# The second projection of a hybrid decoder layer, w_out: half of its inner dimension by Strassen's seven products

## The chip, the core and the metric

The kernel is one program on one core of a Trainium2 chip. Work is done by TensorE (matmuls, PE in the profile, with PEld for the loads of the stationary operand), VectorE (DVE), ScalarE (ACT) and GpSimd (POOL); SyncE (SP) issues most of the transfers from the chip's memory. Each engine works through its own queue of instructions in the order of the built program, and waits at an instruction until what it needs is there. The metric is the device time of one execution in microseconds (us).

## The reference

One decoder layer on 256 tokens of width 1024, all in float32. The part that matters here is the end of the middle sub-layer and the beginning of the last one:

```python
gates = jax.nn.sigmoid(gate_logits + gate_b[l]).reshape(b, L, N_BRANCH, D_MODEL)
merged = gates[:, :, 0] * y_ssd + gates[:, :, 1] * y_att
h = h + rmsnorm(merged @ w_out[l], mix_post_g[l])
h = h + 0.5 * rmsnorm(swiglu(rmsnorm(h, ffn2_pre_g[l]), ffn2_w_gate[l], ffn2_w_up[l], ffn2_w_down[l]),
                      ffn2_post_g[l])
```

`merged` is 256 x 1024 and `w_out` is 1024 x 1024. `y_att` is itself a product with `da_w_branch`.

## The kernel before

**Numbers in two parts.** Every product is made of three: an operand x is split into a rounded part hi (a copy to the type fp32r) and the rest lo = x - hi, and hi*hi, lo*hi and hi*lo are added up in PSUM. For a weight chunk, 1 MB in a raw buffer (`raw`, three of them, filled by SP), ScalarE makes the hi part (`whi`, line 259) and VectorE the lo part (`wlo`, line 260), each in two pieces of 128 x 1024. A raw buffer is free when the second lo piece is made; then SP issues the load of the chunk three further on. `take()` gives the next chunk's two parts and sees that the chunks up to AHEAD = 3 further on are split.

**The stage.** Tokens lie in two blocks b of 128, channels of the output in two halves q of 512. After the attention, `natural("pwd0")` and `natural("pwd1")` multiply with `da_w_branch` (tiles `pwd`, line 382); `merge` (lines 1612, 1613) gates the result and adds the other branch into `gt`; `turn_merged` transposes a block of `merged` on TensorE (tiles `pmg`, line 1596) and splits it into `mh` and `ml` (lines 320, 321). Then `mm_n` multiplies with the four chunks of `w_out` (tiles `acc_mx`, line 676): the first chunk for both blocks and both halves, the other three (held back, TAIL = 3) block by block, half by half, so that a half of a block is done early. Per chunk, block and half there are six matmuls of 512 columns, 96 in all. As each half is done, `norm_half` takes its sum of squares on ScalarE (`jp_mxp`, line 506) and multiplies it by the gain on VectorE (`og_mxp`, line 605); `norm_end` gets the root on GpSimd (`rp_mxp`, lines 511 and 512) and adds to the residual `h` on VectorE (line 645).

**What follows.** For the next sub-layer block 0 of `h` is transposed as it is (`pu_f`, line 520, between matmuls of block 1), split into `u_f` (lines 526, 528) and multiplied with the first four chunks of that sub-layer's weights (tiles `pn_f`, line 382), with its norm applied later. Block 1 of `h` is squared on ScalarE (`sq_f`, line 506), its root is taken on GpSimd (`r_f`, lines 511, 512), VectorE scales it (`un_f`, line 565), and TensorE transposes it (`pu_f` again) after three quarters of block 0's product, that is 36 matmuls of `pn_f`.

**What sets the order.** In this stretch the order of TensorE's queue is the one in which the code is written. ACT's and DVE's queues are ordered by the scheduler of the framework at build time, under a few added constraints: `normed["lo"]` names an instruction behind which the later `wlo` pieces have to stand.

The sub-layers with SwiGLU already use Strassen's scheme for parts of their last product: class `Quad` holds two chunks as four quarters, makes weight sums (`SUMS`), and `mm_quads` runs seven products instead of eight blocks, followed by sums of the results (lines 784 and 787 to 792). `sums_of` makes the sums of the activations.

## Time and profile before

| | us |
|---|---|
| median of 3 runs | 731.69 (731.35 to 731.74) |
| the profiled execution | 731.22 |
| its span, first to last instruction | 729.3 |
| PE busy | 721.3 |
| DVE busy | 608.5 |
| ACT busy | 472.8 |
| the product with `w_out`, first matmul to the first of `pn_f` | 519.71 to 543.36 |

The span lies 1.9 us under the time of the same execution. A row of the timeline has the start and the length in us, the engine, the line, the operation, what it writes and reads, its shape, how many were merged into the row, and in brackets how long the engine was idle before it and what it waited for. The second start in a row of n equal instructions is not shown; the interval between them is the row's length less that of one, divided by n - 1. In the chain of work that ended last, a row is start, length, engine, tile, line and count.

### The profile page before, as it was taken

The page shows a single profiled execution, that of the slowest core. Times are in us where ns is not written, and L with a number is a line of the kernel's source. Part 1 is how long each engine was busy: PE and PEld are TensorE (multiplying, and loading weights), DVE is VectorE, ACT ScalarE, POOL GpSimd, SP SyncE. Part 2 cuts the span into 40 slices and gives each one's busy share as a digit, 9 for nine tenths or more (in the row PEclk, how much of TensorE's full clock was granted, in tenths as well). Part 3 has the DMA queues.
Part 4 walks back from the last instruction along what each step waited for, and adds up shares of the span by engine and source line. Part 5 has one row for each costly group of instructions (what it writes and reads, how often), then busy time and mean ns, then how long its engine had stood idle before and what let it go on. Part 6 is the DMA issues. An engine that isn't in the chain of part 4 may idle for free.

```text
span 729.3 us, 10568 instructions
## 1 busy us (share of the span) xinstructions
PE 721.3 (99%) x4025; PEld 620.5 (85%) x4025; DVE 608.5 (83%) x933; ACT 472.8 (65%) x804; POOL 31.5 (4%) x63
## 2 busy tenths in 40 slices
PE   9999999999999999999999999999999999999996
PEld 8888888888778889999888788888888888888885
DVE  6978788999979989777996998785784878789996
ACT  6657666666867676869965577782563756566562
POOL 4300000000200000000000000000010000000000
PEclk9999999999999999999999999999999999999998
DMA  8884654467674557665564664465461655654551
GB/s 303 229 275 153 208 173 176 170 231 260 185 227 119 172 173 238 208 213 180 155 224 147 205 224 137 152 235 199 120 234 51 230 182 166 231 194 156 174 197 58
DMA packets 94450, 137.92 MB, mean 189 GB/s; under 512 B 2668, under 2 KB 68800, under 8 KB 94400
## 3 DMA queue, kind: packets, MB, share of 16 engines
q1 hardware_dynamic: 91728, 129.51, 53.7%
q0 software_dynamic: 2368, 7.22, 3.3%
q8 instruction: 31, 0.51, 0.3%
q10 hardware_dynamic: 304, 0.53, 0.2%
q14 instruction: 19, 0.16, 0.1%
HBM read 136.17 MB, written 1.08 MB: 188 GB/s over the span
## 4 chain that ended last, share of the span: by engine, by line
PE 95%; DVE 2%; DMA 1%; issue 1%; ACT 0%; DVEq 0%; ACTq 0%
PE pup_f L341 14%; PE pg_f L341 14%; PE pxs L341 6%; PE pws L382 6%; PE pgt L382 6%; PE acc_f2p L755 5%; PE acc_f1p L755 3%; PE pbc L341 3%; PE pk L341 3%; PE pq L341 3%; PE pn_f L398 3%; PE acc_mx L676 3%; PE pn_mx L382 3%; PE pn_f L382 3%; PE pwd L382 3%; PE pz L333 2%
## 5 line engine op out<-in xcount | busy, mean ns | idle before, releaser
L260 DVE TENSOR_TENSOR wlo<-raw,whi 128x1024 fp32r<-128x1024 f32 x216 | 257.0, 1219 | 20.2 <-ACT whi L259 19.0
L259 ACT CAST whi<-raw 128x1024 fp32r<-128x1024 f32 x216 | 218.4, 1049 | 16.1 <-DMA raw<-in_w_in_dram 5.7
L341 PE MATMUL pg_f<-u_f,whi 128*128 128x512 f32 x288 | 69.0, 390 | 0.0
L341 PE MATMUL pup_f<-u_f,whi 128*128 128x512 f32 x288 | 68.7, 391 | 0.0
L341 PEld LDWEIGHTS pg_f<-u_f,whi 128*128 128x128 f32 x288 | 53.9, 188 | 11.1
L341 PEld LDWEIGHTS pup_f<-u_f,whi 128*128 128x128 f32 x288 | 52.9, 188 | 10.2
L130 ACT CAST wqh<-wt 128x1024 fp32r<-128x1024 f32 x24 | 25.2, 1055 | 23.5 <-DVE wt L122 23.4
L341 PEld LDWEIGHTS pg_f<-u_f,wlo 128*128 128x128 f32 x288 | 36.9, 191 | 1.4
L341 PE MATMUL pup_f<-u_f,wlo 128*128 128x256 f32 x288 | 37.5, 283 | 0.0
L341 PE MATMUL pg_f<-u_f,wlo 128*128 128x256 f32 x288 | 37.4, 283 | 0.0
L347 ACT COPY su_f<-pup_f 128x256 f32<-128x256 f32 x36 | 13.2, 372 | 36.1 <-PE pup_f L341 36.1
L341 PEld LDWEIGHTS pup_f<-u_f,wlo 128*128 128x128 f32 x288 | 35.9, 192 | 0.0
L348 DVE TENSOR_TENSOR su_f<-pup_f,su_f 128x256 f32<-128x256 f32 x36 | 15.2, 421 | 24.2 <-ACT su_f L347 24.1
L382 PE MATMUL pgt<-whi,u_mx 128*128 128x512 f32 x128 | 33.1, 393 | 0.0
L341 PE MATMUL pxs<-u_mx,whi 128*128 128x512 f32 x128 | 31.8, 394 | 0.0
L330 PE MATMUL pz<-u_mx,whi 128*128 128x256 f32 x128 | 31.6, 284 | 0.0
L331 PE MATMUL pz<-u_mx,whi 128*128 128x256 f32 x128 | 31.5, 283 | 0.0
L136 DVE TENSOR_TENSOR wql<-wt,wqh 128x1024 fp32r<-128x1024 f32 x24 | 29.1, 1217 | 0.2
L382 PEld LDWEIGHTS pgt<-whi,u_mx 128*128 128x128 f32 x128 | 23.6, 188 | 5.3 <-issue 0.7
L341 PEld LDWEIGHTS pxs<-u_mx,whi 128*128 128x128 f32 x128 | 23.2, 189 | 4.3
L320 ACT CAST gh_f<-sg_f 128x512 fp32r<-128x512 f32 x18 | 11.2, 620 | 23.2 <-DVE sg_f L911 23.2
L136 DVE TENSOR_TENSOR wql<-raw,wqh 128x1024 fp32r<-128x1024 f32 x18 | 21.8, 1219 | 3.5 <-ACT wqh L130 3.5
(415 smaller groups left out, 1585.1 us busy)
## 6 DMA issues: line engine op xcount, KB each, us to landing
raw<-in_w_in_dram SPq DMA_DIRECT2D x40, 1024.0 KB, 5.1
raw<-in_ffn_w_down_dram SPq DMA_DIRECT2D x22, 1024.0 KB, 4.9
raw<-in_ffn_w_gate_dram SPq DMA_DIRECT2D x20, 1024.0 KB, 5.4
raw<-in_ffn_w_up_dram SPq DMA_DIRECT2D x20, 1024.0 KB, 5.2
raw<-in_ssd_w_branch_dram SPq DMA_DIRECT2D x8, 1024.0 KB, 5.0
acb<-acd POOLq DMA_DIRECT2D x8, 512.0 KB, 4.1
raw<-in_da_w_branch_dram SPq DMA_DIRECT2D x4, 1024.0 KB, 5.1
raw<-in_w_out_dram SPq DMA_DIRECT2D x4, 1024.0 KB, 5.1
```

Source lines behind the costliest of these rows:

```text
L130: nc.scalar.copy(hi, src)
L136: nc.vector.tensor_sub(lo, src, hi.bitcast(F32))
L259: last_cast[0] = behind(nc.scalar.copy(hi, r[:, js, :]), "cast").ins
L260: m = nc.vector.tensor_sub(lo, r[:, js, :], hi.bitcast(F32))
L330: nc.tensor.matmul(acc[m], wh(j)[:, cs], ah(k0 + j), start=first and j == ks[0], stop=False)
L331: nc.tensor.matmul(acc[m], wh(j)[:, cs], al(k0 + j), start=False, stop=False)
L341: nc.tensor.matmul(to, w_(j)[:, m * P:(m + 1) * P], x_(j), start=first and j == 0, stop=not first and j == KD - 1, skip_group_check=True)
L348: nc.vector.tensor_tensor(dst, acc[:, :T], dst, ALU.add)
L382: nc.tensor.matmul(acc, a(k0 + j), b(j), start=first and i == 0, stop=last and i == 11)
L398: nc.tensor.matmul(accs[b], x_(k0 + j), w_(j), start=first and j == 0 and w_ is wh and x_ is acts[b][0], stop=last and j == 3 and w_ is wl)
L676: nc.tensor.matmul(acc[b][q][:, cs] if to is None else to, x_[:, ts], w_(kt)[:, halves[q]][:, cs], start=to is not None and kt == 0 and x_ ...
L755: nc.tensor.matmul(bank[p], x_, w_, start=p not in begun, stop=last and p in (1, 5, 6, 7))
```

## The change

The first 512 of the 1024 inner channels of the product with `w_out` are computed by seven products of quarter size (each 128 tokens x 256 channels x 512 outputs, six matmuls) instead of eight. The other two chunks ("plain" chunks) stay as they were. In detail:

- The two chunks 85 and 86 become a `Quad` with the order of products 1, 2, 6, 5, 3, 7, 4. Of the seven weight operands three are quarters of the chunks themselves and four are sums, made on VectorE into one tile `wt_mx` with room for two at a time (it has the tag `u8`, that of the activation buffers that stand idle here); each of the seven is then split (`wqh` on ScalarE, `wql` on VectorE).
- Six of the seven are made ahead, during the products with `da_w_branch`; the sixth in order, product 7, among them, and the seventh, 4, in the middle of the product with `w_out`.
- The merged activations' first half is turned block by block inside `natural("pwd1")`, copied once more in plain form (`mt`) and summed by `sums_of` (`sv`, `sh`, `sl`, `s4`).
- The seven results lie in eight banks of PSUM with the plain chunks' parts and are merged by adds: `p1` copied by ScalarE, `u2`, `u4`, `u3`, `c4` on VectorE, and one more add per half (`half_mixed`) before that half's norm, which then reads its input from SBUF.
- The `wlo` pieces of the next sub-layer's chunks stand behind the second half's add of block 0 (`normed["lo"]`), and those of chunks 91 and 92 are asked for after the halves of block 1.

```diff
@@ -48,6 +48,7 @@
+MIXED = (1, 2, 6, 5, 3, 7, 4)
...
@@ -97,8 +98,8 @@
-        def __init__(self, i, products):
-            self.i, self.sums, self.products = i, {}, products
+        def __init__(self, i, products, homes=None):
+            self.i, self.sums, self.products, self.homes = i, {}, products, homes

...
@@ -118,7 +119,7 @@
             if p not in self.sums:
                 n, m = self.SUMS[p]
                 m = self.sum_of(m) if p in (6, 4) else self.quarter(m, p)
-                t = k4([P, 2, 512], f"wt{self.i}{p}")
+                t = self.homes(p) if self.homes else k4([P, 2, 512], f"wt{self.i}{p}")
                 nc.vector.tensor_sub(t, self.quarter(n, p), m)
                 self.sums[p] = t
             return self.sums[p]
...
@@ -213,8 +214,19 @@
     for c in range(2):
         for k0 in (0, 512):
             s_chunk(da_w_branch[0], k0, c * 512)
-    for c in range(4):
+    sums_home = []
+
+    def mixed_home(p):
+
+        if not sums_home:
+            sums_home.append(sb.tile([P, 4, 2, T], F32, tag="u8", name="wt_mx", bufs=2))
+        return sums_home[0].rearrange("p (a b) c t -> p a b (c t)", a=2)[:, {5: 0, 6: 1, 7: 0, 4: 1}[p]]
+
+    quad(w_out[0], 0, MIXED, mixed_home)
+    last_unit_mx = units.pop()
+    for c in range(2, 4):
         n_chunk(w_out[0], c * 2 * P)
+    units.append(last_unit_mx)
     ffn_chunks("f2", ffn2_w_gate, ffn2_w_up, ffn2_w_down)
 
     raws, splits = [], []
...
@@ -742,6 +754,78 @@
         split(more[:, 0], more[:, 1], v[:, 3])
         return ([hi[:, i] for i in range(3)] + [more[:, 0]], [lo[:, i] for i in range(3)] + [more[:, 1]])
 
+    def of_piece(p, kt, acts, sh, sl):
+
+        if p in (1, 2, 4):
+            k, b = {1: (0, 0), 2: (2, 0), 4: (2, 1)}[p]
+            return [x_[:, b * P:(b + 1) * P] for x_ in acts[k + kt]]
+        return [x_[{5: 0, 6: 1, 7: 2, 3: 3}[p]][:, kt, :] for x_ in (sh, sl)]
+
+    def mm_mixed(acts, sums, turn_next, half, done, turned):
+
+
+        bank, begun = {}, set()
+        sh, sl = sums
+        rest = {n: k2([P, 512], f"{n}_mx") for n in ("p1", "u2", "u4", "u3", "c4")}
+        add = lambda o, p, u: nc.vector.tensor_tensor(rest[o], bank[p], rest[u], ALU.add)
+
+        def mm(p, x_, w_, stop):
+            nc.tensor.matmul(bank[p], x_, w_, start=p not in begun, stop=stop)
+            begun.add(p)
+
+        def piece(p, w):
+            if p not in bank:
+                bank[p] = pj(f"acc_mxp{p}") if p in (1, 6, 7, 4) else bg([P, 512], f"acc_mxp{p}")
+            wh, wl = w
+            for kt in range(2):
+                ah, al = of_piece(p, kt, acts[:4], sh, sl)
+                for x_, w_ in ((ah, wh), (al, wh), (ah, wl)):
+                    mm(p, x_, w_(kt), kt == 1 and w_ is wl and p in (1, 5, 6, 7))
+
+        def plain(b, q, p, i, w, at):
+            wh, wl = w
+            for kt in range(2):
+                if (i, kt) == at:
+                    turned()
+                ah, al = (x_[:, b * P:(b + 1) * P] for x_ in acts[4 + 2 * i + kt])
+                for x_, w_ in ((ah, wh), (al, wh), (ah, wl)):
+                    mm(p, x_, w_(kt)[:, halves[q]], i == 1 and kt == 1 and w_ is wl)
+
+        def part(b, q, p, ws, o, at=None):
+            for i, w in enumerate(ws):
+                plain(b, q, p, i, w, at)
+            return half(b, q, bank[p], rest[o])
+
+        split_to(taken[0] + 7)
+        piece(1, take(0))
+        nc.scalar.copy(rest["p1"], bank[1])
+        piece(2, take(0))
+        piece(6, take(0))
+        turn_next()
+        add("u2", 6, "p1")
+        piece(5, take(0))
+        turn_next()
+        add("u4", 5, "u2")
+        piece(3, take(0))
+        w7 = take(0)
+        ws = [take(1) for _ in range(2)]
+        split_to(taken[0] + 1)
+        w4 = take(0)
+        part(0, 0, 2, ws, "p1")
+        normed["lo"] = part(0, 1, 3, ws, "u4")
+        done(0)
+        split_to(ahead_of(taken[0], AHEAD - 2))
+        split_to(ahead_of(taken[0], AHEAD - 1))
+        piece(7, w7)
+        add("u3", 7, "u2")
+        add("c4", 5, "u3")
+        piece(4, w4)
+        bank[8] = pj("acc_mxp8")
+        part(1, 0, 4, ws, "u3", at=(1, 1))
+        part(1, 1, 8, ws, "c4")
+        split_to(ahead_of(taken[0], AHEAD))
+        done(1)
+
     def mm_quads(acts, sums, tag):
 
 
...
@@ -1541,18 +1621,20 @@
 
     own_order(PE)
 
-    def natural(name, n, hi, lo, evict, us, then=lambda: None):
+    def natural(name, n, hi, lo, evict, us, then=lambda: None, ahead={}, behind_block=lambda i: None):
 
 
         accs = [pj(f"{name}{b}") for b in range(2)]
         for i in range(n):
-            w = take()
+            w = take(2 if i in ahead else AHEAD)
+            split_to(taken[0] + ahead.get(i, 0))
             for b in range(2):
                 bs = slice(b * P, (b + 1) * P)
                 mm_nat(accs[b], w, (lambda k: hi(k)[:, bs], lambda k: lo(k)[:, bs]), i * 4, i == 0, i == n - 1, "u")
                 if i == n - 1:
                     evict(b, accs[b])
                 back.run(us)
+                behind_block(i)
             if i == 0:
                 then()
 
...
@@ -1586,49 +1668,64 @@
     yh = yl = None
     while turned_pairs[0] < 2:
         back.run(0.1)
-    mg, merges = [], []
+    mg, merges, turned_halves, plain_mg, sums_mg = [], [], [], [], []
 
     def turn_merged(n):
 
-        for q, b, t, mh, ml in merges[:n]:
+        for q, b, t in merges[:n]:
+            if len(turned_halves) == q:
+                turned_halves.append([k4([P, 4, T], f"m{x_}{q}", F32R) for x_ in "hl"])
+                mg.extend((turned_halves[q][0][:, m, :], turned_halves[q][1][:, m, :]) for m in range(4))
+            mh, ml = turned_halves[q]
             pt = bg([P, 4, P], f"pmg{q}{b}")
             for m in range(4):
                 nc.tensor.transpose(pt[:, m, :], t[:, m * P:(m + 1) * P], ident)
             bs = slice(b * P, (b + 1) * P)
             split(mh[:, :, bs], ml[:, :, bs], pt)
+            if q == 0:
+                nc.scalar.copy(plain_mg[0][:, :, bs], pt)
         del merges[:n]
 
     def attended():
         back.drain()
         act_table(SILU)
 
+    def turn_block(i):
+        if i == 0:
+            turn_merged(1)
+            if not merges:
+                sums_mg.append(sums_of(0, plain_mg[0][:, 0:2, :], plain_mg[0][:, 2:4, :]))
+
     for q in range(2):
-        mh = k4([P, 4, T], f"mh{q}", F32R)
-        ml = k4([P, 4, T], f"ml{q}", F32R)
-        mg += [(mh[:, m, :], ml[:, m, :]) for m in range(4)]
-
         def merge(b, acc):
             t0, t1 = gt[0][b][:, halves[q]], gt[1][b][:, halves[q]]
             nc.vector.tensor_tensor(t1, acc, t1, ALU.mult)
-            nc.vector.tensor_tensor(t1, t1, t0, ALU.add)
-            merges.append((q, b, t1, mh, ml))
-
+            m = nc.vector.tensor_tensor(t1, t1, t0, ALU.add)
+            if (q, b) == (1, 0):
+                normed["lo"] = m.ins
+            merges.append((q, b, t1))
+
+        if q == 1:
+            plain_mg.append(k4([P, 4, T], "mt"))
         natural(f"pwd{q}", 2, lambda j: oh[j // 4][:, j % 4, :], lambda j: ol[j // 4][:, j % 4, :], merge,
-                SSD_US if q == 0 else 0.0, (attended, lambda: turn_merged(2))[q])
+                SSD_US if q == 0 else 0.0, (attended, lambda: None)[q], ({}, {0: 7, 1: 6})[q],
+                (lambda i: None, turn_block)[q])
 
     pg = load_gain(mix_post_g, "pg_mx")
-    acc = [[bg([P, 512], f"acc_mx{b}{q}") for q in range(2)] for b in range(2)]
 
     made, ready, turned = next_norm("f2", "f2")
+    norms_mx = [{}, {}]
+
+    def half_mixed(b, q, acc, rest):
+        m = nc.vector.tensor_tensor(rest, acc, rest, ALU.add)
+        norm_half(norms_mx[b], b, q, rest, pg, 1.0, "mxp")
+        return m.ins
 
     def mixed(b):
-        n = {}
-        for q in range(2):
-            norm_half(n, b, q, acc[b][q], pg, 1.0, "mxp")
-        norm_end(n, b, 1.0, "mxp")
+        norm_end(norms_mx[b], b, 1.0, "mxp")
         ready(b)
 
-    mm_n(acc, mg, mixed, turned, lambda: turn_merged(1))
+    mm_mixed(mg, sums_mg[0], lambda: turn_merged(1), half_mixed, mixed, turned)
 
 
     norm = made[0]
```

What it does to the queues, at three places. The names are those of the two builds; chunk 90 is `raw90`, its pieces `wlo900` and `wlo901`.

DVE, from the first half of block 1's norm (`og_mxp10`) to the scaled block 1 (`un_f211`), before:

```order
L605 TENSOR_TENSOR og_mxp10_5457<-acc_mx10_5242,pg_mx_5238 128x512
L528 SCALAR_TENSOR_TENSOR u0_f2_5352<-pu_f200_5392,cols_a_112,u0_f2_5352 128x128 x4
L528 SCALAR_TENSOR_TENSOR u1_f2_5353<-pu_f201_5405,cols_a_112,u1_f2_5353 128x128 x4
L260 TENSOR_TENSOR wlo920_5483<-raw92_5362,whi920_5482 128x1024
L260 TENSOR_TENSOR wlo921_5487<-raw92_5362,whi921_5486 128x1024
L605 TENSOR_TENSOR og_mxp11_5461<-acc_mx11_5243,pg_mx_5238 128x512
L645 SCALAR_TENSOR_TENSOR h_72<-og_mxp10_5457,rp_mxp1_5463,h_72 128x512
L645 SCALAR_TENSOR_TENSOR h_72<-og_mxp11_5461,rp_mxp1_5463,h_72 128x512
L565 TENSOR_SCALAR un_f210_5476<-h_72,r_f21_5473 128x512
L565 TENSOR_SCALAR un_f211_5478<-h_72,r_f21_5473 128x512
```

And in the changed kernel, from the same instruction on:

```order
L617 TENSOR_TENSOR og_mxp10_5478<-u3_mx_5269,pg_mx_5264 128x512
L617 TENSOR_TENSOR og_mxp11_5495<-c4_mx_5270,pg_mx_5264 128x512
L272 TENSOR_TENSOR wlo910_5498<-raw91_5343,whi910_5497 128x1024
L272 TENSOR_TENSOR wlo911_5502<-raw91_5343,whi911_5501 128x1024
L657 SCALAR_TENSOR_TENSOR h_72<-og_mxp10_5478,rp_mxp1_5507,h_72 128x512
L657 SCALAR_TENSOR_TENSOR h_72<-og_mxp11_5495,rp_mxp1_5507,h_72 128x512
L272 TENSOR_TENSOR wlo920_5527<-raw92_5399,whi920_5526 128x1024
L272 TENSOR_TENSOR wlo921_5531<-raw92_5399,whi921_5530 128x1024
L577 TENSOR_SCALAR un_f210_5520<-h_72,r_f21_5517 128x512
L577 TENSOR_SCALAR un_f211_5522<-h_72,r_f21_5517 128x512
```

Between the gain of the last half and the update of `h` now stand `wlo910` and `wlo911`, and `wlo920` and `wlo921` between `h` and `un_f`.

Ahead of that, DVE in the changed kernel from the second half of block 0 on (`u4`, which is line 1720; the results of products 7, 5, 4 and 8 are `acc_mxp7` and so on):

```order
L1720 TENSOR_TENSOR u4_mx_5268<-acc_mxp3_5328,u4_mx_5268 128x512
L272 TENSOR_TENSOR wlo890_5392<-raw89_5176,whi890_5391 128x1024
L617 TENSOR_TENSOR og_mxp01_5382<-u4_mx_5268,pg_mx_5264 128x512
L272 TENSOR_TENSOR wlo891_5396<-raw89_5176,whi891_5395 128x1024
L657 SCALAR_TENSOR_TENSOR h_72<-og_mxp00_5365,rp_mxp0_5384,h_72 128x512
L657 SCALAR_TENSOR_TENSOR h_72<-og_mxp01_5382,rp_mxp0_5384,h_72 128x512
L272 TENSOR_TENSOR wlo900_5402<-raw90_5279,whi900_5401 128x1024
L272 TENSOR_TENSOR wlo901_5406<-raw90_5279,whi901_5405 128x1024
L770 TENSOR_TENSOR u3_mx_5269<-acc_mxp7_5411,u2_mx_5267 128x512
L540 SCALAR_TENSOR_TENSOR u0_f2_5389<-pu_f200_5437,cols_a_112,u0_f2_5389 128x128
L770 TENSOR_TENSOR c4_mx_5270<-acc_mxp5_5313,u3_mx_5269 128x512
L540 SCALAR_TENSOR_TENSOR u0_f2_5389<-pu_f200_5437,cols_a_112,u0_f2_5389 128x128 x3
```

From here to `og_mxp10` above stand four more of `u1_f2` and two adds of line 1720 (`u3_mx` with `acc_mxp4`, `c4_mx` with `acc_mxp8`). Before, `og_mxp00`, two `wlo`, `og_mxp01` and two `h` stood in this place, followed by `og_mxp10`.

ACT, the last halves' sums of squares and the squares of `h`, before:

```order
L506 ACTIVATE jp_mxp10_5455,sp_mxp1_5454<-acc_mx10_5242 128x512
L526 ACTIVATE u0_f2_5352<-pu_f200_5392,cols_a_112 128x128 x4
L526 ACTIVATE u1_f2_5353<-pu_f201_5405,cols_a_112 128x128 x4
L259 CAST whi920_5482<-raw92_5362 128x1024
L259 CAST whi921_5486<-raw92_5362 128x1024
L506 ACTIVATE jp_mxp11_5459,sp_mxp1_5454<-acc_mx11_5243 128x512
L506 ACTIVATE sq_f210_5469,ss_f21_5468<-h_72 128x512
L506 ACTIVATE sq_f211_5471,ss_f21_5468<-h_72 128x512
L415 ACTIVATE sg_f2b0_5581<-pn_f200_5492,r_f20_5423 128x512
```

and now:

```order
L271 CAST whi910_5497<-raw91_5343 128x1024
L518 ACTIVATE jp_mxp10_5476,sp_mxp1_5475<-u3_mx_5269 128x512
L518 ACTIVATE jp_mxp11_5493,sp_mxp1_5475<-c4_mx_5270 128x512
L271 CAST whi911_5501<-raw91_5343 128x1024
L271 CAST whi920_5526<-raw92_5399 128x1024
L518 ACTIVATE sq_f210_5513,ss_f21_5512<-h_72 128x512
L271 CAST whi921_5530<-raw92_5399 128x1024
L518 ACTIVATE sq_f211_5515,ss_f21_5512<-h_72 128x512
L427 ACTIVATE sg_f2b0_5625<-pn_f200_5536,r_f20_5468 128x512
```

`whi911` and `whi920` now stand between the last sum of squares and the first square of `h`, and `whi921` between its two squares.

10 lines of the change are left out of this document (3 added, 7 removed).

## The prediction

> **What bounds the kernel now.** I read the page first, then the chain of waits around the product with `w_out`, then the queues of the other engines there. The page's busy times and its chain by engine:
>
> ```profile
> PE 721.3 (99%) x4025; PEld 620.5 (85%) x4025; DVE 608.5 (83%) x933; ACT 472.8 (65%) x804; POOL 31.5 (4%) x63
> PE 95%; DVE 2%; DMA 1%; issue 1%; ACT 0%; DVEq 0%; ACTq 0%
> ```
>
> TensorE is the bound nearly everywhere: a matmul taken away is time gained, if nothing holds TensorE instead. The chain from the product with `w_out` to the next sub-layer (start, length, count):
>
> ```profile
> 513.54 0.87 PE pmg L1596 x8
> 514.42 5.46 PE pwd L382 x24
> 519.87 2.73 PE acc_mx L676 x12
> 522.60 0.44 PE pmg L1596 x4
> 523.04 2.76 PE acc_mx L676 x12
> 525.80 0.44 PE pmg L1596 x4
> 526.23 12.29 PE acc_mx L676 x54
> 538.53 0.87 PE pu_f L520 x8
> 539.40 4.13 PE acc_mx L676 x18
> 543.53 8.16 PE pn_f L382 x36
> 551.69 0.87 PE pu_f L520 x8
> ```
>
> There is no wait in it (each piece starts where the last matmul before it ends, hence 543.53 where `pn_f` starts at 543.36): matmuls of 512 columns follow each other at 12.29 / 54 = 0.228 us, four transposes take 0.44. The question is which hand-over to TensorE comes late once it is faster. The last `pu_f`, block 1's, needs `un_f`, the end of a chain over four engines. Its rows on ACT, POOL and DVE, then TensorE's:
>
> ```profile
> 543.62 0.60 ACT L506 ACTIVATE jp_mxp<-acc_mx 128x512 f32<-128x512 f32 x1 [0.36 <-PE acc_mx L676]
> 544.12 0.19 ACT L506 ACTIVATION_READ_ACCUMULATOR jp_mxp<-acc_mx 128x1 f32 x1
> 544.41 0.57 POOL L511 TENSOR_SCALAR rp_mxp<-sp_mxp 128x1 f32<-128x1 f32 x1 [4.69 <-ACT jp_mxp L506]
> 545.66 1.42 DVE L645 SCALAR_TENSOR_TENSOR h<-og_mxp,rp_mxp,h 128x512 f32<-128x512 f32 x2 [0.25 <-POOL rp_mxp L512]
> 546.51 0.63 ACT L506 ACTIVATE sq_f<-h 128x512 f32<-128x512 f32 x1 [2.19 <-DVE h L645]
> 547.17 0.63 ACT L506 ACTIVATE sq_f<-h 128x512 f32<-128x512 f32 x1
> 547.99 0.30 POOL L511 TENSOR_SCALAR r_f<-ss_f 128x1 f32<-128x1 f32 x1 [2.36 <-ACT sq_f L506]
> 548.97 1.03 DVE L565 TENSOR_SCALAR un_f<-h,r_f 128x512 f32<-128x512 f32 x2 [1.89 <-POOL r_f L512]
> 551.53 1.03 PE L520 MATMUL pu_f<-ident,un_f 128*128 128x128 f32 x8
> ```
>
> The first `un_f` is done at 548.97 + 0.55 = 549.52 and TensorE takes it at 551.53: 2.0 us of slack. In this chain DVE and ACT are idle when their turn comes (the brackets), so it runs at its shortest.
>
> **The change part by part.** *Taken from TensorE:* 48 matmuls of the first two chunks become 42. All 16 transposes `pmg` stay; two groups of four with matmuls between them cost 0.88, eight in one piece 0.87. Gain 6 x 0.228 = 1.37 us, and block 1's `pu_f` is reached at 551.53 - 1.37 = 550.16. Slack left, were the chain unmoved: 2.0 - 1.4 = 0.6.
>
> *Added ahead of the product:* on DVE four weight sums and three more `wql` (seven with four `wlo`, where eight `wlo` stood), 7 pieces of 1.14 us = 8.0 us, and the activation sums and their split, some 2.5 us; on ACT three more pieces of 0.95, two copies `mt` and the two splits, some 5 us. What stood there:
>
> ```profile
> 505.42 0.69 DVE L1612 TENSOR_TENSOR gt<-pwd,gt 128x512 f32<-128x512 f32 x1 [5.59 <-PE pwd L382]
> 514.63 1.29 DVE L321 TENSOR_TENSOR ml<-pmg,mh 128x512 fp32r<-128x512 f32 x2 [5.08 <-ACT mh L320]
> 514.02 1.07 ACT L320 CAST mh<-pmg 128x512 fp32r<-128x512 f32 x2 [16.11 <-PE pmg L1596]
> ```
>
> Idle time of 5.6 and 5.1 us on DVE and 16.1 on ACT covers it: DVE's weight work from 499 to 510 delays the gated halves by about a microsecond, and their transposes come only at 510.7 and 513.8. I cost it at nothing. The cover ends about 521, where DVE still has `wlo` pieces of the plain chunks to make, with the adds between: from the bank of product 5, full at 519.87 + 24 x 0.228 + 0.44 = 525.8, an add 0.60, `wlo880` 1.14, `ml` 0.60 and `wlo881` 1.23 (intervals below) make 529.4; the 42nd matmul, which reads it, starts at 519.71 + 41 x 0.228 + 0.88 = 529.9, 0.5 us later. That is the tightest place ahead of the end.
>
> *Moved transfers:* the fourth `w_out` chunk's load, the last in the first row below, now waits for the last weight sum (about 506 instead of 500), is there 5.1 us later and is first read about 525; the loads of the next sub-layer's chunks behind it move with their `wlo` pieces, the last by some 7 us, to about 552.
>
> ```profile
> 483.66 16.60 SPq L241 DMA_DIRECT2D raw<-in_w_out_dram  x4
> raw<-in_w_out_dram SPq DMA_DIRECT2D x4, 1024.0 KB, 5.1
> 544.84 0.37 SPq L241 DMA_DIRECT2D raw<-in_ffn_w_gate_dram  x1
> 564.70 2.95 ACT L259 CAST whi<-raw 128x1024 fp32r<-128x1024 f32 x3
> ```
>
> That chunk is the last of the three then loaded and is not opened before 567: hidden. The gain vector's load on POOL, which waits for a later matmul of `pwd` (about 513 instead of 503), is read at 531, and POOL has nothing else before 534: hidden, too.
>
> *The end, which decides.* The second half of block 0 is now ready for DVE when the 54th matmul ends: 519.87 + 54 x 0.228 + 2 x 0.44 = 533.06. From there DVE has no pause. Intervals (a row's length less one instruction's, over n - 1):
>
> ```profile
> 528.66 3.49 DVE L260 TENSOR_TENSOR wlo<-raw,whi 128x1024 fp32r<-128x1024 f32 x3
> 540.38 2.16 DVE L528 SCALAR_TENSOR_TENSOR u_f<-pu_f,cols_a,u_f 128x128 fp32r<-128x128 f32 x8 [0.34 <-ACT u_f L526]
> 174.73 1.29 DVE L784 TENSOR_TENSOR u_f<-acc_f1p,u_f 128x512 f32<-128x512 f32 x2
> 526.88 2.95 ACT L259 CAST whi<-raw 128x1024 fp32r<-128x1024 f32 x3
> ```
>
> So 1.14 us for a `wlo`, 0.26 for a `u_f`, 0.60 for an add of two 128 x 512 (an add of a bank, the same kind as here, and `og` likewise), 0.66 for `h` (1.42 x 2), and on ACT 0.95 for a `whi`. DVE's queue from `u4` on, as in the order shown: u4 0.60, wlo 1.14, og 0.60, wlo 1.14, two h 1.32, two wlo 2.28, u3 0.60, u_f 0.26, c4 0.60, seven u_f 1.82, u3 0.60: 10.96, so the last add `c4` starts at 544.0, 1.9 us after its bank is full (543.53 - 1.37 = 542.16), and is done at 544.7. Then ACT: the last half's `jp` starts 544.8 and its sum is there 0.69 later (543.62 to 544.31 above); POOL needs 1.35 to `h` (544.31 to 545.66): 546.8. But DVE is at the two `og` to 545.8 and at `wlo910` and `wlo911` to 548.1, so `h` starts at 548.1, 1.3 us late. From the start of `h` to `un_f` took 548.97 - 545.66 = 3.31, and now `whi921` stands between the two squares: + 0.95. `un_f` starts at 548.1 + 3.31 + 0.95 = 552.4 and is done 0.55 later. TensorE resumes at 552.9 instead of 551.53.
>
> **Sum:** TensorE arrives at 550.16, waits 2.75 us and goes on 1.4 us later than before. Some four hand-offs between engines that the intervals leave out (0.03 to 0.1 each, like 544.31 to 544.41 above) and the second `un_f` (0.48 behind the first, while four transposes take 0.44) add 0.1 to 0.3: I take + 1.6. Everything behind is TensorE's again, in the same order, so nothing gives it back. 731.22 of the profiled execution + 1.6 = 732.8; this execution lies 0.47 under the median, so 733.3. Bounds of the unknown (how far DVE's queue is packed): with no queue at all the wait vanishes, - 1.37; with each of DVE's some 20 steps 0.06 longer, + 2.6.
>
> **What a wait of 2.8 us does to the clock** no row here shows in the middle of the program; the nearest are the only gap between matmuls, and the end:
>
> ```profile
> 183.66 1.32 PE L520 MATMUL pu_mx<-ident,h 128*128 128x128 f32 x8 [0.87 <-DVE h L645]
> 182.80:183.66 0.86, 0.00 (x0) 0.00 (x0) 0.86 (x3) 0.67 (x1) 0.00 (x0) 1.00 0.51 38
> 722.15:723.26 1.11, 1.11 (x10) 0.91 (x8) 1.07 (x4) 0.22 (x1) 0.00 (x0) 1.00 0.00 0
> 723.26:725.56 2.30, 0.00 (x1) 0.00 (x0) 1.95 (x6) 1.08 (x5) 0.00 (x0) 1.00 0.00 0
> 725.57:729.28 3.71, 0.00 (x0) 0.00 (x0) 0.77 (x2) 0.00 (x0) 0.00 (x0) 0.50 0.37 141
> ```
>
> The column behind POOL is the granted clock. A gap of 0.86 us, in which TensorE waits for the `h` of the norm before (the first row), left it at 1.00; 2.30 us after the last matmul it fell to 0.50. Our 2.8 us lie between and beyond. [...]
>
> **The rivals.**
> 1. *Half clock behind the wait.* For it: the rows just shown. Against: the 0.86 us gap. If the clock stays halved for about as long as it takes to fall (from the 2.30 us above to the 3.3 us of the longest wait I expect), TensorE loses half of that, 1.2 to 1.6 us: 734.5 to 734.9, I take 734.8. It may hit some executions and not others.
> 2. *The wait stays away: faster.* If `un_f` is ready by 550.2, 2.8 us earlier than I make it, all 1.37 us are kept: 731.69 - 1.37 = 730.3. Place: DVE between the banks' adds and `h`; it decides from where DVE has caught up when the last bank (8) is full. For it: DVE had pauses of 0.25 to 1.89 us in these rows. Against: the change puts four adds of combination, two of halves and four `wlo` (9 us) where the pauses were 2 to 4 us together.
> 3. *A wait ahead of the end as well.* If `wlo881` is later than by my 0.5 us of margin, TensorE waits there and the whole end moves along, one for one: 0.5 to 1.5 us more, about 734.3. Against: by the same reckoning DVE, after `wlo881` (529.3), a `wql` 1.14, an add and an `og`, is through at 531.6 and pauses 1.4 us for the bank of 533.06, so it isn't overfull there.
>
> **How the numbers follow.** What a measurement of this kernel can tell from no change is about 0.2%, 1.46 us: below 730.2 is faster, above 733.15 slower. My forecast (wait without a halved clock, 732.6 to 734.0): 0.50, of which about a third lies under 733.15. Rival 1: 0.31. Rival 2: 0.09. Rival 3: 0.10, a few hundredths of it with a shorter end. So faster 0.09, same 0.20, slower 0.71. The range leaves out rival 2 and the far end of rivals 1 and 3: 731.5 to 735.8.
>
> **What would show it.** `pn_f` would begin at 542.0 instead of 543.36 (step one); between the 36th `pn_f` and block 1's `pu_f` TensorE idle for 2 to 3.3 us, put down to DVE `un_f`; DVE without a pause over 0.2 us from 533 to 549, `h` directly behind a `wlo`; no other gap of TensorE over 0.2 us from 500 to 550. Granted clock 1.00 in the 4 us behind the wait, or 0.50 for rival 1. I am wrong if `un_f` starts before 550, if the gap lies in another place, or if the later FFN products get closer together and give the time back.

## The result and the profile after

The changed kernel takes 736.27 us in the median of four runs (735.54 to 737.35), the kernel before 731.52 beside it: ratio on record 1.0072, 95% interval 1.0059 to 1.0084 (the bare quotient of the two medians, 1.0065, lies inside it). It is slower by about 5 us where 1.6 were forecast, and lies outside the range (735.8 at its upper end). The profiled execution is the slowest of the four, 737.35 with a span of 735.6.

Busy times of the page, then the chain of waits around the end of the product (start, length, engine, tile, line, count):

```profile
PE 723.5 (98%) x4019; PEld 621.9 (85%) x4019; DVE 624.1 (85%) x954; ACT 478.8 (65%) x812; POOL 35.0 (5%) x63
PE 90%; DVE 5%; issue 2%; ACT 1%; DMA 1%; POOL 1%; DVEq 0%; ACTq 0%; POOLq 0%
```

```profile
520.26 4.08 PE acc_mxp L773 x18
...
533.48 0.70 DVE u_mx L1720
...
535.03 0.98 POOL rp_mxp L523
...
536.08 1.40 POOL rp_mxp L524
...
546.67 2.72 POOL rp_mxp L523
...
555.31 1.97 PE pu_f L532 x8
...
```

Before, the chain stayed on TensorE here. Now it leaves it at 533.48 and returns at 555.31: for 22 us the chain that ends last runs over the other engines. The product begins 0.39 later than before (520.26 against 519.87, a delay that goes back to the first 8 us of the program); this has to be taken off each start below when it is compared with the forecast. TensorE's own rows, with its idle time in brackets:

```profile
538.40 1.29 PE L532 MATMUL pu_f<-ident,h 128*128 128x128 f32 x8 [0.20 <-DVE h L657]
...
542.96 1.07 PE L394 MATMUL pn_f<-whi,u_f 128*128 128x512 f32 x4
...
555.31 1.97 PE L532 MATMUL pu_f<-ident,un_f 128*128 128x128 f32 x8 [4.04 <-DVE un_f L577]
```

The gap is where it was forecast, at block 1's `pu_f` for `un_f`, but it is 4.04 us long instead of 2.75. A smaller one stands at block 0's `pu_f`. In the chain the eye falls on POOL: the addition of two numbers per token (`rp_mxp`, line 523) takes 2.72 us where it took 0.57. POOL's rows there, and DVE's beside them:

```profile
535.03 0.97 POOL L523 TENSOR_SCALAR rp_mxp<-sp_mxp 128x1 f32<-128x1 f32 x1 [20.77 <-ACT jp_mxp L518]
536.08 1.39 POOL L524 TENSOR_TENSOR rp_mxp<-rp_mxp,small 128x1 f32<-128x1 f32 x1
542.78 0.31 POOL L523 TENSOR_SCALAR r_f<-ss_f 128x1 f32<-128x1 f32 x1 [5.32 <-ACT sq_f L518]
...
546.67 2.71 POOL L523 TENSOR_SCALAR rp_mxp<-sp_mxp 128x1 f32<-128x1 f32 x1 [2.94 <-ACT jp_mxp L518]
549.46 0.56 POOL L524 TENSOR_TENSOR rp_mxp<-rp_mxp,small 128x1 f32<-128x1 f32 x1
553.28 0.70 POOL L523 TENSOR_SCALAR r_f<-ss_f 128x1 f32<-128x1 f32 x1 [3.26 <-ACT sq_f L518]
```

```profile
535.22 0.69 DVE L617 TENSOR_TENSOR og_mxp<-u_mx,pg_mx 128x512 f32<-128x512 f32 x1
535.82 1.22 DVE L272 TENSOR_TENSOR wlo<-raw,whi 128x1024 fp32r<-128x1024 f32 x1
537.50 1.42 DVE L657 SCALAR_TENSOR_TENSOR h<-og_mxp,rp_mxp,h 128x512 f32<-128x512 f32 x2 [0.47 <-POOL rp_mxp L524]
...
542.65 1.89 DVE L540 SCALAR_TENSOR_TENSOR u_f<-pu_f,cols_a,u_f 128x128 fp32r<-128x128 f32 x7
...
545.06 0.68 DVE L1720 TENSOR_TENSOR c_mx<-acc_mxp,c_mx 128x512 f32<-128x512 f32 x1
545.66 0.68 DVE L617 TENSOR_TENSOR og_mxp<-u_mx,pg_mx 128x512 f32<-128x512 f32 x1
546.25 0.69 DVE L617 TENSOR_TENSOR og_mxp<-c_mx,pg_mx 128x512 f32<-128x512 f32 x1
546.86 2.35 DVE L272 TENSOR_TENSOR wlo<-raw,whi 128x1024 fp32r<-128x1024 f32 x2
550.05 1.41 DVE L657 SCALAR_TENSOR_TENSOR h<-og_mxp,rp_mxp,h 128x512 f32<-128x512 f32 x2 [0.84 <-POOL rp_mxp L524]
551.38 2.43 DVE L272 TENSOR_TENSOR wlo<-raw,whi 128x1024 fp32r<-128x1024 f32 x2
554.66 1.02 DVE L577 TENSOR_SCALAR un_f<-h,r_f 128x512 f32<-128x512 f32 x2 [0.84 <-POOL r_f L524]
```

Read the ends together. POOL's addition ends at 536.00, 549.38 and 553.98; DVE's `og` ends at 535.91, its two `wlo` at 549.21, the next two at 553.81: each time POOL is through 0.1 to 0.2 us after an operation of DVE that takes both inputs from SBUF. Behind each pair of `wlo` DVE pauses. Behind that `og` the next `wlo` follows directly, so there POOL came through at a border within the run, and why it did so there and not between two `wlo` is not shown. Beside `u_f`, which takes one input from PSUM, the addition needs 0.31 (at 542.78). And three times DVE then waits for POOL: 0.47, 0.84 and 0.84.

Last, the clock. Columns: window, its length, busy time of PE, PEld, DVE, ACT and POOL, the granted clock, the transfers' share and GB/s.

```profile
549.99:553.40 3.41, 1.29 (x6) 0.75 (x4) 3.35 (x4) 2.50 (x6) 0.15 (x2) 1.00 0.88 266
553.40:556.81 3.41, 1.50 (x7) 1.50 (x8) 1.44 (x3) 0.70 (x3) 1.92 (x3) 0.50 0.61 174
556.81:560.23 3.42, 3.42 (x11) 2.75 (x10) 2.16 (x8) 1.83 (x8) 0.00 (x0) 0.50 0.52 180
560.23:563.64 3.41, 3.41 (x17) 2.78 (x16) 0.75 (x1) 0.00 (x0) 0.00 (x0) 1.00 0.00 0
```

In the window from 549.99 TensorE was busy for 1.29 of 3.41 us, and the clock fell at its end; in the next it was busy for 1.50, and the clock stayed at half through the one behind, in which TensorE makes 11 matmuls instead of 17.

### The profile page after: what moved, and what is told of

Its sections match the earlier page's. It is cut to its first block, busy times and chain, and to the rows that moved or that the text cites. A ratio compares the mean times of both kernels' runs of the same rounds, so it can differ in the third digit from the quotient of the medians.

```text
span 735.6 us, 10592 instructions
## 1 busy us (share of the span) xinstructions
PE 723.5 (98%) x4019; PEld 621.9 (85%) x4019; DVE 624.1 (85%) x954; ACT 478.8 (65%) x812; POOL 35.0 (5%) x63
## 4 chain that ended last, share of the span: by engine, by line
PE 90%; DVE 5%; issue 2%; ACT 1%; DMA 1%; POOL 1%; DVEq 0%; ACTq 0%; POOLq 0%
PE pup_f L353 14%; PE pg_f L353 14%; PE pxs L353 6%; PE pws L394 6%; PE pgt L394 6%; PE acc_f2p L839 5%; PE pbc L353 3%; PE pn_f L410 3%; PE pk L353 3%; PE pq L353 3%; PE pn_mx L394 3%; PE pwd L394 3%; PE pz L345 2%; PE pz L343 2%; PE pz L342 2%; PE pn_f L394 2%
## 5 line engine op out<-in xcount | busy, mean ns | idle before, releaser
L272 DVE TENSOR_TENSOR wlo<-raw,whi 128x1024 fp32r<-128x1024 f32 x212 | 253.0, 1222 | 18.5 <-ACT whi L271 18.1
L271 ACT CAST whi<-raw 128x1024 fp32r<-128x1024 f32 x212 | 214.9, 1048 | 15.2 <-DMA raw<-in_w_in_dram 4.7
L137 DVE TENSOR_TENSOR wql<-raw,wqh 128x1024 fp32r<-128x1024 f32 x21 | 25.5, 1220 | 3.6 <-ACT wqh L131 3.6
```

What stands on the lines that cost most here:

```text
L137: nc.vector.tensor_sub(lo, src, hi.bitcast(F32))
L271: last_cast[0] = behind(nc.scalar.copy(hi, r[:, js, :]), "cast").ins
L272: m = nc.vector.tensor_sub(lo, r[:, js, :], hi.bitcast(F32))
```

## The experiments

The theory: the whole loss is two waits on tiles of `h` plus the price of the halved clock, and the waits are long because POOL cannot run its small additions beside DVE's subtractions. Against it stand that Strassen's additional work on DVE alone makes the wait, wherever POOL stands; that the clock costs nothing of its own; and that any late `un_f` would do the same without Strassen. For each run the table gives the ratio to the kernel before with its interval, TensorE's wait at block 1's `pu_f`, for how long the clock stood at 0.50 behind it, and the time from that `pu_f` to the end of the span. TensorE's work in that last column is the same in all of these runs, so what it has over 177.75 is the price of the clock.

| kernel | ratio (95%) | wait, us | at 0.50, us | `pu_f` to end, us |
|---|---|---|---|---|
| before | 1 | 0 | 0 | 729.28 - 551.53 = 177.75 |
| changed | 1.0072 (1.0059 to 1.0084) | 4.04 | 6.83 | 735.65 - 555.31 = 180.34 |
| changed, 30 products of zeros | 1.0075 (1.0063 to 1.0088) | 0 | 0 | 177.78 |
| changed, 14 products of zeros | 1.0044 (1.0032 to 1.0056) | 0.92 | 0 | 177.91 |
| changed, last two `wlo` ahead of `h` | 1.0089 (1.0075 to 1.0103) | 5.00 | 3.41 | 179.55 |
| changed, last two `wlo` behind `un_f` | 1.0045 (1.0033 to 1.0058) | 2.73 | 3.41 | 179.60 |
| changed, roots on ACT | 1.0013 (1.0005 to 1.0022) | 1.76 | 0 | 177.83 |
| before, six products of `h` | 1.0055 (1.0042 to 1.0068) | 2.92 | 3.41 | 179.42 |
| before, four products of `h` | 1.0023 (1.0013 to 1.0034) | 1.45 | 0 | 177.86 |

**What the clock costs.** TensorE is given products of zeros (into the bank that the transposes overwrite) in the place of the wait, first thirty, then fourteen:

```diff
-        pu = bg([P, 4, P], f"pu_{name}{b}{q}")
+        pu = bg([P, 4, P], f"pu_{name}{b}{q}"); [nc.tensor.matmul(pu[:, 0, :], zeros, zeros, start=True, stop=True) for _ in range(14) if (name, b, q) == ("f2", 1, 0)]
```

> The changed kernel with thirty products of a 128 x 128 tile of zeros put on TensorE directly ahead of block 1's first pu_f (30 x 0.106 us = 3.2 us, in the bank that the transposes then overwrite), so that TensorE works for most of the time in which it waited for un_f. Nothing else moves. Theory (the loss is the wait for un_f plus a halved clock behind it): pu_f still starts when un_f is there, the clock stays at 1.00 behind it, and the time falls by the price of the halved clock, 2.0 to 2.8 us of 736.3: 733.5 to 734.3. Rival (the halved clock is a sign of the wait and costs nothing of its own, or comes from something else): 736.3 as before.

> As the kernel with thirty products of zeros, now with fourteen, since each took 0.222 us and not 0.106: 3.1 us of filling in a wait of 4.0. Theory: pu_f starts when un_f is there, the clock stays at 1.00, and what is left against the kernel before is the wait less the six matmuls, 4.0 - 1.4 = 2.7 us, ratio 1.0037. Rival (no price of the clock): the ratio stays at the changed kernel's 1.0072.

TensorE's rows with thirty and with fourteen (each product is two matmuls in the profile):

```profile
549.40 6.86 PE L530 MATMUL pu_f<-zeros 128*128 128x128 f32 x60
556.10 1.04 PE L532 MATMUL pu_f<-ident,un_f 128*128 128x128 f32 x8
```

```profile
550.26 3.29 PE L530 MATMUL pu_f<-zeros 128*128 128x128 f32 x28
554.46 1.09 PE L532 MATMUL pu_f<-ident,un_f 128*128 128x128 f32 x8 [0.92 <-DVE un_f L577]
```

Thirty were too many by my own costing: they took 6.7 us, and `pu_f` starts at 556.10 where it could have started at 553.6 (`un_f` from 552.94 on, and the 0.65 that lies between the two above), 2.5 us later. That the time is still that of the changed kernel says that a halved clock costs as much as those 2.5 us. Fourteen leave `pu_f` to `un_f`, the clock stays at 1.00, and the ratio falls from 1.0072 to 1.0044 although TensorE gets `un_f` no sooner: the rival is out. In the last column the halved clock costs 2.59 us where it stood for 6.83, in the first half of which TensorE worked for only 1.50, and 1.7 to 1.85 where it stood for 3.41.

**Whether Strassen is needed for it.** The kernel before, with products of `h` by 1.0 on DVE ahead of block 1's squares:

```diff
-                made[0].unit1(tag == "mx")
+                [nc.vector.tensor_scalar(h[:, 1, :], h[:, 1, :], 1.0, None, ALU.mult) for _ in range(6 if tag == "f2" else 0)]; made[0].unit1(tag == "mx")
```

> The kernel before, without Strassen's products, with six products of h's second block with 1.0 on DVE ahead of the second norm (the values stay as they are): some 6.1 us that delay un_f, 2.0 of them covered. Theory (a late un_f costs its wait and a halved clock behind it, whatever made it late): TensorE waits 4.1 us at block 1's pu_f, the clock falls to 0.50 for one or two stretches of 3.4 us, time + 5.9 to 6.7 us, ratio 1.0081 to 1.0092. Rival (the wait costs itself only): + 4.1, ratio 1.0056.

> The kernel before with four products of h's second block with 1.0 ahead of the second norm instead of six: 4 x 0.73 = 2.9 us. Theory: TensorE waits 1.4 to 1.6 us at block 1's pu_f, which is too short for the clock to fall; time + 1.5 us, ratio 1.0020. Rival (any such wait halves the clock for 3.4 us): + 3.3, ratio 1.0045.

The windows of the kernel with six, and TensorE's row of the one with four:

```profile
550.96:554.38 3.42, 0.50 (x4) 0.08 (x2) 0.92 (x3) 1.91 (x5) 1.55 (x3) 1.00 0.00 0
554.38:557.79 3.41, 3.41 (x12) 3.09 (x13) 1.45 (x6) 2.18 (x8) 0.08 (x1) 0.50 0.03 5
```

```profile
551.98 1.09 PE L520 MATMUL pu_f<-ident,un_f 128*128 128x128 f32 x8 [1.45 <-DVE un_f L565]
```

Each product took 0.73 us and not the 1.0 that I had costed, so six made a wait of 2.92 instead of 4.1. The measured ratio therefore meets the rival's figure by accident: with the wait that there was, the rival gives 2.92 / 730.7 = 1.0040 and the theory, with 1.7 for the clock, 1.0063. The interval (1.0042 to 1.0068) holds the theory's figure and leaves the rival's just outside, which is a narrow margin; the halved clock in the windows and the 179.42 of the table decide. Four give a wait of 1.45, a full clock, and nothing beyond the wait, as expected.

**What makes `un_f` late.** Three kernels. First one more chunk is split ahead of block 1's norm, which puts four `wlo` in a row between `og` and `h` and leaves nothing between `h` and `un_f`:

```diff
-        split_to(ahead_of(taken[0], AHEAD))
+        split_to(ahead_of(taken[0], AHEAD + 1))
         done(1)
```

> The changed kernel with one more chunk split ahead of the second norm: the last two wlo of the next sub-layer's first chunks (and both their whi) stand ahead of block 1's h, where they stood between h and un_f (and one whi between the two squares). On DVE four wlo in a row stand between og and h, and nothing between h and un_f. Theory 1 (POOL's little add for the root cannot run while DVE subtracts one SBUF tensor from another): the add lasts until the fourth wlo ends, about 4.9 us instead of 2.7, h starts 0.8 later than the last wlo at 552.3, the root of the squares runs in 0.3 + 0.6 with DVE idle, un_f at 555.5, 0.8 later than in the changed kernel; time 736.5 to 737.5. Theory 2 (POOL's add is slow by a fixed amount): it lasts 2.7 us, h follows the fourth wlo at 551.5, un_f at 554.8, time 736.3. By the prediction's own sum, in which the whi between the squares cost 0.95 and POOL nothing: h 2.3 later, 0.95 back, un_f 1.3 later.

```profile
545.73 4.98 POOL L523 TENSOR_SCALAR rp_mxp<-sp_mxp 128x1 f32<-128x1 f32 x1 [2.94 <-ACT jp_mxp L518]
...
553.71 0.30 POOL L523 TENSOR_SCALAR r_f<-ss_f 128x1 f32<-128x1 f32 x1 [2.36 <-ACT sq_f L518]
```

```profile
545.91 4.63 DVE L272 TENSOR_TENSOR wlo<-raw,whi 128x1024 fp32r<-128x1024 f32 x4
551.38 1.42 DVE L657 SCALAR_TENSOR_TENSOR h<-og_mxp,rp_mxp,h 128x512 f32<-128x512 f32 x2 [0.84 <-POOL rp_mxp L524]
```

The addition lasts 4.98 us, until 0.17 after the fourth `wlo` (4.9 expected), and 0.30 with DVE idle. A fixed slowness would have been 2.7 again. Second, the same two `wlo` and their casts go behind:

```diff
-        nc.scalar.activation(junk, src, AF.Square, scale=(fold / D) ** 0.5, accum_out=ss)
+        unit_done["sq"] = nc.scalar.activation(junk, src, AF.Square, scale=(fold / D) ** 0.5, accum_out=ss).ins
...
-            ws = [take(1) for _ in range(4)]
+            ws = [normed.update(lo=last_unit[0], cast=unit_done["sq"]) or take(1) for _ in range(4)] if self.tag == "f2" else [take(1) for _ in range(4)]
```

> The changed kernel with the last two wlo behind un_f and both their whi behind the squares, so that between h and un_f DVE and ACT do nothing else. Theory 1 (POOL's add waits for DVE's subtractions): its second add, for the root of the squares, runs beside an idle DVE in 0.3 instead of 0.7 us, and without the whi between the squares un_f starts at 553.2 instead of 554.7; TensorE waits 2.6 us instead of 4.0; up to 0.5 us comes back as a wait for the late wlo. Time 734.8 to 735.5 with a halved clock, 732.5 to 733.3 if 2.6 us leave the clock alone. Rival (what is late ahead of h alone decides, the steps between h and un_f are hidden): 736.3.

The second root's addition takes 0.30 again, the wait falls to 2.73 and the ratio to 1.0045 (734.8 to 735.5 of 731.5 is 1.0045 to 1.0055): with the halved clock, as expected. Third, the roots leave POOL:

```diff
-            r = rstd_of(n["ss"], fold, f"rp_{tag}{b}")
+            n["e"] = n.get("e") or tiny(1, f"ep_{tag}{b}"); nc.scalar.activation(n["e"], n["ss"][:, 0:1], AF.Identity, bias=eps_c); r = rstd_act(n["ss"], n["e"], f"rp_{tag}{b}")
...
-                made[0].unit1(tag == "mx")
+                made[0].unit1(True)
...
-        act_table(SILU)
+
...
-    norm = made[0]
+    norm = made[0]; act_table(SILU)
```

> The changed kernel with the roots of the mix's norm (both blocks) and of block 1's second norm on ACT, as logarithm and exponential, where POOL had them; ACT keeps that table until the first Silu behind. Theory (POOL's adds wait for DVE's subtractions): h of block 1 follows the second wlo directly, 0.8 earlier, and un_f follows the fourth wlo, 1.7 earlier in all; TensorE's wait falls from 4.0 to 2.4 us, its wait of 0.2 for block 0's h goes or stays; ratio 1.0045 to 1.0055 with a halved clock, 1.0015 to 1.0025 without. Rival (DVE's queue alone decides): h and un_f stay where they are, ratio 1.0072.

```profile
544.67 2.53 DVE L272 TENSOR_TENSOR wlo<-raw,whi 128x1024 fp32r<-128x1024 f32 x2
547.13 1.40 DVE L657 SCALAR_TENSOR_TENSOR h<-og_mxp,rp_mxp,h 128x512 f32<-128x512 f32 x2
548.45 2.37 DVE L272 TENSOR_TENSOR wlo<-raw,whi 128x1024 fp32r<-128x1024 f32 x2
550.96 0.88 DVE L577 TENSOR_SCALAR un_f<-h,r_f 128x512 f32<-128x512 f32 x2
```

Now `h` stands directly behind a `wlo` with no bracket, as the prediction had it, and `un_f` directly behind the next two. The wait is 1.76 us, the clock stays, and the ratio is 1.0013: better than expected (1.0015 to 1.0025). POOL's share of the loss, the 0.3 and 0.56 us that its own two steps need included, is thus 4.04 - 1.76 = 2.3 us of waiting, and the clock on top. What remains is put down to DVE's queue; two of its adds are left out of that kernel:

```diff
-        add("u3", 7, "u2")
-        add("c4", 5, "u3")
...
-        part(1, 0, 4, ws, "u3", at=(1, 1))
-        part(1, 1, 8, ws, "c4")
+        part(1, 0, 4, ws, "u2", at=(1, 1))
+        part(1, 1, 8, ws, "p1")
```

> The kernel with the roots on ACT, without the two adds that form block 1's rests from products 7 and 5 (u3, c4; block 1's halves are then added to older rests, so two of Strassen's combinations are left out of the result): 2 x 0.60 us less on DVE between block 0's h and the last add. Theory (what is left of the wait is DVE's queue, one for one): un_f 1.2 us earlier, TensorE's wait 1.76 falls to about 0.6, ratio 0.9995 to 1.0000. Rival (the last bank or the casts on ACT set the end, not the number of DVE's steps): the wait stays within 0.4 us, ratio 1.0010 or above.

The wait fell by 1.32, from 1.76 to 0.44 us, but not for one reason. The build order that came out put another `wlo` ahead of block 0's `h`, so TensorE waited 0.78 there instead of 0.25 and came some 0.5 later to block 1's `pu_f`; `un_f` itself started 0.83 earlier (32.67 us behind the start of the last `pwd` matmul with the adds, 31.83 without), not 1.2. The ratio, 1.0009 (1.0000 to 1.0018), hardly moved. So fewer adds on DVE do bring `un_f` forward, but not one for one, and by the time the test decides nothing.

**Whether the gain can be had.** The first of these kernels moves block 1's transposes behind 12 more matmuls that don't need them; the next two add the roots on ACT, with the lo weights last in the third and fourth quarters, the transposes behind all twelve or behind eight of them. The diff is that of the first:

```diff
-        evict, {3: [norm.turns1], 5: [norm.settle, norm.rescale], 7: [lambda: back(0)]}))
+        evict, {4: [norm.turns1], 5: [norm.settle, norm.rescale], 7: [lambda: back(0)]}))
```

> The changed kernel with block 1's eight transposes behind the fourth quarter of block 0's product instead of ahead of it: 12 matmuls, 2.7 us, that do not need un_f stand in the place of the wait. Theory (the loss is the wait and the clock behind it, and the time taken from TensorE is otherwise kept): pu_f starts at about 555.2 with waits of together 1.2 us (0.4 and 0.8 for the two late wlo), the clock stays at 1.00, time 731.5 - 1.4 + 1.2 = 731.3. Rival 1 (block 1's product then waits for its own u_f, 0.5 to 1.0 us): 731.8 to 732.3. Rival 2 (Strassen's additional work on DVE holds TensorE at a later place just as long): 735 or more.

> The kernel with the roots on ACT, and block 1's transposes behind the fourth quarter of block 0's product, whose third and fourth quarters now end with the lo weights instead of having them in the middle. Theory (Strassen's gain of 1.4 us is real and hidden by the wait alone): no wait of TensorE over 0.3 us from 500 to 570, clock 1.00, 0.2 to 0.5 us left of the waits: ratio 0.9982 to 0.9988. Rival (DVE's extra work of some 9 us comes due at some other place): ratio 1.000 or above.

> The kernel with the roots on ACT and block 1's transposes behind the eighth of the twelve matmuls of block 0's last quarter; block 0's transposes where they were, the orders of DVE and ACT as with the roots alone. Theory: the wait of 1.76 us is filled by 8 x 0.228 = 1.82 us of matmuls, block 1's product finds its u_f ready, what stays is block 0's late h (0.6 us): ratio 0.9983 to 0.9990. Rival (a new wait for the lo weights or for u_f of 0.5 us or more): 0.9991 or above.

The move alone gives 1.0018 (1.0009 to 1.0027), above the 0.9997 expected. `pu_f` no longer waits, but TensorE does, for the cast that stands between the two squares, which the expectation had not counted:

```profile
551.65 0.74 PE L394 MATMUL pn_f<-whi,u_f 128*128 128x512 f32 x2 [0.89 <-ACT whi L271]
...
554.41 1.04 PE L532 MATMUL pu_f<-ident,un_f 128*128 128x128 f32 x8
```

With the roots on ACT it is 0.9991 (0.9982 to 0.9999) and 0.9992 (0.9983 to 1.0001): some 0.6 us under the kernel before, not quite half of the six matmuls, and the best that was found. Both gain less than was expected (0.9982 to 0.9988 and 0.9983 to 0.9990), and with intervals that end at 0.9999 and 1.0001 the gain is hardly clear of noise. Four more kernels went after the other half. The first, second and fourth of them have block 0's transposes three matmuls later, for its late `h`; the second, third and fourth have the last two `wlo` behind `un_f`, with their casts ahead of the squares; the fourth leaves the roots on POOL. The diff shows the two moves of the transposes, without the moved `wlo` and casts:

```diff
-                        mm_nat(acc, ws[2 * i + c], act, c * 4, c == 0, c == 1, "u")
+                        mm_nat(acc, ws[2 * i + c], act, c * 4, c == 0, c == 1, "w" if n in (2, 3) and self.tag == "f2" else "u", {8: self.turns1} if n == 3 and self.tag == "f2" else {})
...
-        part(1, 0, 4, ws, "u3", at=(1, 1))
-        part(1, 1, 8, ws, "c4")
+        part(1, 0, 4, ws, "u3")
+        part(1, 1, 8, ws, "c4", at=(0, 0))
...
```

> The kernel with the roots on ACT; block 1's transposes behind the eighth of the twelve matmuls of block 0's last quarter (its third and fourth quarters end with the lo weights), and block 0's transposes three matmuls later, so that h of block 0 is there. Theory: TensorE waits nowhere over 0.15 us from 500 to 570, and nearly all of the six matmuls is kept: ratio 0.9975 to 0.9985. Rival (the DVE order that results, with one wlo moved ahead of block 1's h, makes un_f late again by about 1.1 us): 0.9990 to 1.0005.

> Roots on ACT; both groups of transposes later (block 0's by three matmuls, block 1's behind the eighth matmul of block 0's last quarter); and the last two wlo behind un_f, their whi ahead of the squares, so that between h and un_f nothing else stands on DVE or ACT. Theory (the loss is made of waits for two late tiles, h of block 0 and un_f, and of the clock; Strassen's other work on DVE is covered): no wait over 0.15 us from 500 to 570, all six matmuls kept: 1.2 to 1.4 us under the kernel before, ratio 0.9981 to 0.9984. Rival (DVE's 9 us more are not covered and come due wherever the waits are cleared): 0.9990 or above, with a new wait of 0.5 us or more at the lo weights or at block 1's u_f.

> As before it, but block 0's transposes stay where they were: theory: the wait of 0.6 us for block 0's h stays, nothing else: 0.7 to 0.8 us under the kernel before, ratio 0.9988 to 0.9991. Rival: 0.9995 or above.

> The same two moves of the transposes and the last two wlo behind un_f, but with all roots on POOL as in the changed kernel. Theory (POOL's adds wait for DVE's subtractions): the root of block 1's mix norm still waits for the wlo ahead of h (0.8 us), the one of the squares runs beside an idle DVE in 0.3 us; un_f comes 0.5 to 1.0 later than with the roots on ACT, TensorE waits 0.3 to 1.0 us: ratio 0.9985 to 0.9996. Rival (POOL's stretch is of no account once the order is right): as the first, 0.9981 to 0.9984.

Measured: 0.9996 (0.9987 to 1.0004), 1.0008 (1.0000 to 1.0017), 1.0001 (0.9992 to 1.0010) and 1.0029 (1.0019 to 1.0039). In the first three the rival was right; the fourth lies above both of its figures. With block 0's transposes later, `pn_f` starts 22.46 us behind the last `pwd` matmul where it was 23.88 before (23.09 in the changed kernel): 1.4 us sooner, so the six matmuls are there in full. But then TensorE stands 0.68 us for `un_f` (the first of the four), or twice for the lo weights:

```profile
552.11 0.73 PE L394 MATMUL pn_f<-wlo,u_f 128*128 128x512 f32 x2 [0.44 <-DVE wlo L272]
553.24 0.73 PE L394 MATMUL pn_f<-wlo,u_f 128*128 128x512 f32 x2 [0.40 <-DVE wlo L272]
```

(the second of the four). DVE's busy time, third in the row, from the end of block 0's half to block 1's transposes, in the kernel before, the changed one and that second one:

```profile
533.00:551.50 18.50, 18.50 (x87) 15.35 (x86) 12.54 (x21) 10.56 (x27) 4.69 (x9) 1.00 0.58 198
```

```profile
533.00:551.30 18.30, 18.04 (x82) 14.26 (x81) 16.52 (x26) 10.77 (x25) 6.49 (x6) 1.00 0.47 149
```

```profile
531.50:551.40 19.90, 19.90 (x97) 16.47 (x95) 17.87 (x29) 15.87 (x39) 4.10 (x3) 1.00 0.54 177
```

68% before, 90% after, and 90% with the waits for block 0's `h` and for `un_f` cleared. In this stretch DVE has become nearly as full as TensorE, and in each of these orders the tile that was pulled forward pushed another one back. POOL with the same order costs 1.0029 - 1.0008, some 1.5 us: the direction that the theory gave, but more than its 0.3 to 1.0 us, since TensorE waits 1.44 us for `un_f`, besides the same two waits for the lo weights.

## Why the prediction was right in kind and wrong in size

Two steps of the sum failed. The chain from the last sum of squares to `h`, put at the 1.35 us that it took before, was lengthened by POOL waiting for DVE, and TensorE's wait became 4.04 us instead of 2.75. And the halved clock, which the sum put at nothing and left to a rival, came with that wait and cost 2.59 us in the profiled execution. That a wait of about 2.8 us leaves the clock alone is shown by no run: behind 2.73 us (the last two `wlo` behind `un_f`) it stood at 0.50 for 3.41, behind 1.76 (the roots on ACT) it stayed at 1.00. A smaller third one, a wait for block 0's `h`, took 0.58 of the gain.

- *The place and the direction*: right. The loss starts as a wait of TensorE at block 1's `pu_f` for `un_f`; of its 4.04 us 1.76 are there without POOL's roots and go with DVE's queue behind Strassen's adds. The weight sums ahead of the product, the moved transfers and `wlo881` held nothing up, as costed.
- *Step one, `pn_f` at 542.0*: 542.96, less the late begin 542.57. It gained 0.79 of the 1.37. Missing is a wait that the prediction did not have, for block 0's `h`: 0.20 in the bracket, and as much again inside the eight transposes, whose row is 1.29 long. POOL's root of block 0 took 0.97 and 1.39, before 0.47 and 0.57.
- *DVE's packed queue to the last add, 544.0*: 545.06 - 0.39 = 544.67. The 0.47 that DVE waited for that same root is most of the difference; the intervals themselves were right.
- *"POOL needs 1.35 to `h`"*: the term that failed. The addition waited for the two `wlo` that the sum itself had put beside it: 2.71 and 0.56 instead of 0.57 and 0.56. So `h` did not stand directly behind a `wlo` at 548.1 but at 549.66 (550.05 less 0.39), with DVE idle for 0.84 ahead of it. The sign stood in the rows before: the prediction said that the chain ran at its shortest there, but the same addition took 0.57 for `rp_mxp` and 0.30 for `r_f`, and the longer one, from 544.41, ended at 544.98, 0.17 after this pair:

```profile
542.46 2.35 DVE L260 TENSOR_TENSOR wlo<-raw,whi 128x1024 fp32r<-128x1024 f32 x2
```

The 3.31 from `h` to `un_f` held the same mistake, 0.70 for 0.30. Without POOL in the chain the sum is about right: by it, and with the wait of block 0 in, TensorE would arrive at 550.9 and have `un_f` at 552.9, a wait of 2.0; the kernel with the roots on ACT has 1.76.
- *The cast between the squares, + 0.95*: right, a row of ACT's in the chain.
- *Rival 1, the halved clock*: it came true, with 0.31 given to it, and dearer than worked out, 2.59 in the profiled execution against 1.2 to 1.6: 3.41 us at 0.50 cost 1.7 to 1.85 in three other kernels, and here it stood for 6.83. The length of the wait alone does not give that: the kernel with four `wlo` in a row waited 5.00 us and had 3.41. The mistake was to let the clock stay halved for about as long as it takes to fall: it fell 2.1 us after the last matmul here (551.27 to 553.40) and stayed low for 6.83. The two rows of the end that the prediction shows are 1.11 us of matmuls from 722.15 and 2.30 of idle time, so TensorE was busy for a third of the 3.41 us ahead of that fall, as in the middle of the program now (1.29). Idle time of 2.30 us did not always do it: with four `wlo` in a row the clock held for 5.3 us behind the last matmul (550.34 to 555.65).
- *The sum with the measured terms*: - 0.79 + 4.04 + 2.59 = 5.84. The spans differ by 735.65 - 729.28 = 6.37; 0.39 is the begin, 0.14 is left. The other three executions are 0.7 to 1.8 us shorter, at a mean granted clock of 0.995 against 0.994 here; how much of that is a shorter half clock and how much the begin of the program was not settled.
- *The range*: the two cases that were kept apart, a wait longer than the sum and a halved clock, came together: the halved clock was there with the waits of 2.73 us and more, and not with those of 1.76 and less.
